# Attention of a two-layer decoder trunk: the transposes of both heads' probabilities moved beside those of the values, and a pair's outputs beside the scores of a later pair

## The chip, the cores and the metric

One core of one Trainium2 chip runs the whole program in one launch. The metric is the device time of one execution in microseconds (us). The kernel before has a median of 549.41 us over 3 runs (549.16 to 550.0).

## What is computed

The reference is a trunk of two layers over 256 tokens of width 1024, in float32: layer 0 mixes by causal pooling, layer 1 by attention, and each is followed by a squared-ReLU MLP. The change touches the attention of layer 1 alone. With 256 tokens there is one key block, so its sparse attention is plain causal attention over 16 heads of 64, with a bias by distance (cut):

```python
qkv = h @ w_qkv
logit = einsum('bhqd,bhkd->bhqk', q, k) * scale + bias_own      # causal: -inf above the diagonal
p = softmax(logit, axis=-1)
out = einsum('bhqk,bhkd->bhqd', p, v)
return out.reshape(B, S, D) @ w_o
```

## The kernel before, in words

All weights stream from memory and are split into a high and a low part (`w..._hi` by ACT on L247, `w..._lo` by DVE on L252), eight 128x128 tiles at a time and three such halves ahead of their use. A product with one weight tile is one **step**: three matmuls (L271 to L273). `next_tile()` counts the steps. `later(d, fn)` puts a function `d` steps on; what is due at a step is issued ahead of its three matmuls, in the order in which it was entered. Each engine runs its instructions in the order in which they were issued, so these numbers set the order of the work on PE, ACT and DVE, and nothing else does.

The products with `w_qkv` are 24 outputs of 8 steps. The heads go in eight pairs, and the outputs come in the order q, k of pair p, then v of pair p - 1, so that a pair takes 24 steps. The class `Pair` (from L898) hangs the attention of pair p between those steps:

- `done`: DVE takes an output out of its PSUM bank (L441, L443), and ACT turns it into q, k or the transposed v (L916: `qk`, `vT`).
- `scores` (10 steps after k): four matmuls in PE tiles of 64 rows and 128 columns into the banks `sc..._0` and `sc..._1` (L929). Then, spaced by steps, DVE adds the bias and takes the row maximum (`logits`, L944 and L949), ACT takes the exponentials with their sums (`exp`, L955), DVE the reciprocals (L960), and ACT multiplies by them (`normalize`, L966). The result stands in the tiles `L..._0` and `L..._1`.
- `transposes(e)` (25 and 26 steps after the scores): head e's probabilities are turned by three PE transposes into a bank `pt..._e` (L972). One step on, ACT copies them out to `PT..._e` (L974).
- `values` (9 steps after v is done): two PE transposes into the bank `pv` (L982), one step on ACT's copy to `v` (L984).
- `have`, called by both: when all is there, `outputs` follows 9 steps later, 5 for the last pair. It is four matmuls in PE tiles of 128 rows and 64 columns into the bank `po` (L996, L997), two steps on ACT's copy of the high part `ol` (L1001), one step on DVE's low part (L1004).

All banks come from one pool of eight. After the 192 steps of `w_qkv` the product with `w_o` begins. Its first five outputs `wo0` to `wo4` run side by side for 40 steps and hold five banks all that time, while the last two pairs are still being finished. Step counts below are from the scores of the pair, or of `w_o`.

Of the kernel before, what the change touches and what calls it, by code (L numbers as in the profile page):

```python
# [23 lines left out]
NP = H // 2  # L24
# [116 lines left out]
def tile_hybrid_pool_moba(  # L141
# [24 lines left out]
    def bank(name):  # L166
        return ps.tile([P, 512], F32, tag="ps", name=name)

    def al_tile(shape, name, dt=F32):
        return act.tile(shape, dt, tag="al", bufs=KF, name=name)  # L170
# [268 lines left out]
    def unnormed_out(b, R, name):  # L439
        u = tmp.tile([P, S], F32, tag="u", bufs=5, name=f"{name}_u")  # L440
        nc.vector.tensor_mul(u, b[:, :S], R)  # L441
        e = tmp.tile([P, 1], F32, tag="b", bufs=4, name=f"{name}_b")
        nc.vector.tensor_reduce(e, b[:, S:LO], axis=AX.X, op=ALU.add)  # L443
        return u, e
# [217 lines left out]
    def later(d, fn):  # L662
        due.setdefault(now[0] + d, []).append(fn)
# [22 lines left out]
    def up(layer, hl, R):  # L686
# [54 lines left out]
        for n, k in UP_ORDER[layer]:  # L741
            w = next_tile()
            paired = R is None and n < g and n % 2 == 1
            if k == 0:
                banks[n] = banks[n - 1] if paired else bank(f"{name}{n}")
            t = hl[k]
            if R is None:
                a = S if paired else 0

                last = n % 2 == 1 or n >= g  # L750
                args = (banks[n][:, a : a + S], w, t[:, :S], t[:, S : 2 * S], k == 0 and a == 0, k == KD - 1 and last)

                if k == 0 and n < HALF:
                    first_tiles.append(args)
                    if n == HALF - 1:
                        mm_sums(first_tiles)
                else:
                    mm_sum(*args)
            else:
                mm_sum(banks[n][:, :LO], w, t[:, :LO], t[:, LO : LO + S], k == 0, k == KD - 1)  # L760
            if k == KD - 1:
                done(n)
# [135 lines left out]
    class Pair:  # L898
# [15 lines left out]
        def done(self, j, b):  # L914
            u, e = unnormed_out(b, R[0], f"qkv{self.p}_{j}")
            later(1, lambda: nc.scalar.activation(self.dst(j), u, AF.Identity, bias=e))  # L916
            if j == 1:
                later(10, self.scores)
            if j == 2:
                later(9, self.values)  # L920

        def scores(self):
            p = self.p
            self.sc = [bank(f"sc{p}_{e}") for e in range(2)]
            for t in range(2):
                n = (t + 1) * P
                for e in range(2):
                    rows = slice(e * DH, (e + 1) * DH)
                    nc.tensor.matmul(  # L929
                        self.sc[e][:, t * P : t * P + n], self.qk[rows, 0, t * P : (t + 1) * P],  # L930
                        self.qk[rows, 1, S - n :], start=True, stop=True,
                    )
            self.prob = [al_tile([P, 2, (t + 1) * P], f"L{p}_{t}") for t in range(2)]
            for i, (t, e) in enumerate(((0, 0), (0, 1), (1, 0), (1, 1))):
                later(2 + i, lambda t=t, e=e: self.logits(t, e))
                later(10 + i, lambda t=t, e=e: self.exp(t, e))
                later(16 + i, lambda t=t, e=e: self.normalize(t, e))
            later(25, lambda: self.transposes(0))
            later(26, lambda: self.transposes(1))

        def logits(self, t, e):
            n = (t + 1) * P
# [43 lines left out]

        def have(self):
            if self.v is not None and len(self.PT) == 2:
                later(9 if self.p < NP - 1 else 5, self.outputs)

        def outputs(self):
            p = self.p
# [21 lines left out]
    for i, (n, k) in enumerate(QKV_ORDER):  # L1014
        w = next_tile()
        p, j = divmod(n, 3)
# [149 lines left out]
```

## Time and profile before

| what | us |
|---|---|
| median of 3 runs | 549.41 |
| the profiled execution, whole | 550.51 |
| its span (first to last instruction) | 548.7 |
| PE busy, share of the span | 537.5, 98% |
| DVE busy | 410.5, 75% |
| ACT busy | 323.6, 59% |
| the products with `w_qkv` on PE | 238.2 to 329.4 |
| the products with `w_o` begin | about 329.5 |

The profiled execution took 1.1 us longer than the median of the runs; 1.8 us of it lie around the span. Busy times of PE are of overlapping matmuls: a matmul is listed with some 0.28 us, and the next one starts 0.12 us after it. So what PE loses is read from start to start, not from its busy share.

### The profile page before, as it was taken

What the parts mean: (1) busy time and instruction counts of PE and PEld (TensorE: products, weight loads), DVE (VectorE), ACT (ScalarE), POOL (GpSimd) and SP (SyncE); (2) the same over time, 40 slices, a digit from 0 to 9 for tenths busy, and PEclk for the clock granted to TensorE, in tenths of its full rate; (3) what the DMA queues carried; (4) which work ended last, traced back from release to release, by engine and by line L of the source; (5) the groups of instructions that cost most, each with busy time, mean ns of one, the idle gap of its engine ahead of it and who ended that gap; (6) DMA issues with size and microseconds to landing.
All of it is one profiled execution on the core that took longest, in us unless ns stands there. A gap on an engine that the chain in (4) does not pass through costs nothing.

```text
span 548.7 us, 11124 instructions
## 1 busy us (share of the span) xinstructions
PE 537.5 (98%) x4492; PEld 499.5 (91%) x4492; DVE 410.5 (75%) x830; ACT 323.6 (59%) x605; POOL 2.5 (0%) x18
## 2 busy tenths in 40 slices
PE   8998999999999999999999999999999999999995
PEld 7777999999988888999999899999999998888895
DVE  2865598799889889966999994777887786665541
ACT  4224335789744445546988778566997774444531
POOL 1000000000000000000000000000000000000000
PEclk9997999999999999999999999999999999999998
DMA  8999989468999988974558774353565567676002
GB/s 335 416 420 406 360 321 380 177 231 300 318 383 392 382 334 324 351 254 153 189 213 297 289 288 163 121 206 141 177 226 173 212 230 260 221 263 254 1 1 76
DMA packets 22339, 140.43 MB, mean 256 GB/s; under 512 B 2416, under 2 KB 4608, under 8 KB 5904
## 3 DMA queue, kind: packets, MB, share of 16 engines
q1 hardware_dynamic: 22048, 138.61, 67.8%
q10 hardware_dynamic: 144, 1.05, 0.5%
q8 instruction: 35, 0.57, 0.4%
q14 instruction: 16, 0.13, 0.1%
q0 software_dynamic: 96, 0.06, 0.0%
HBM read 138.64 MB, written 1.07 MB: 255 GB/s over the span
## 4 chain that ended last, share of the span: by engine, by line
PE 92%; DMA 6%; DVE 0%; issue 0%; ACT 0%; DVEq 0%; ACTq 0%
PE m1d L264 9%; PE m0d L264 9%; PE m1u L271 6%; PE m1u L272 6%; PE m1u L273 6%; PE m0u L271 5%; PE m0u L273 5%; PE m0u L272 5%; PE m1d L265 5%; PE m0d L265 5%; PE qkv L271 5%; PE qkv L272 4%; PE qkv L273 4%; DMA raw_c_sh<-in_w_mod 3%; DMA raw_c_g<-in_w_mod 2%; PE wo L271 1%
## 5 line engine op out<-in xcount | busy, mean ns | idle before, releaser
L252 DVE TENSOR_TENSOR w_lo<-raw_w,w_hi 128x1024 fp32r<-128x1024 f32 x160 | 194.6, 1223 | 59.5 <-ACT w_hi L247 57.8
L247 ACT CAST w_hi<-raw_w 128x1024 fp32r<-128x1024 f32 x160 | 166.4, 1047 | 76.6 <-PE m1d L264 25.0
L264 PE MATMUL m1d<-m1u_al,w_hi 128*128 128x512 f32 x224 | 78.7, 394 | 0.0
L264 PE MATMUL m0d<-m0u_al,w_hi 128*128 128x512 f32 x224 | 78.1, 392 | 0.0
L295 DVE SCALAR_TENSOR_TENSOR raw_m<-raw_m,cact 128x1024 f32<-128x1024 f32 x62 | 75.3, 1218 | 0.0
L271 PE MATMUL m1u<-h_raw,w_hi 128*128 128x258 f32 x256 | 72.8, 284 | 0.0
L272 PE MATMUL m1u<-h_raw,w_hi 128*128 128x256 f32 x256 | 72.6, 284 | 0.0
L273 PE MATMUL m1u<-h_raw,w_lo 128*128 128x258 f32 x256 | 72.5, 283 | 0.0
L271 PE MATMUL m0u<-h,w_hi 128*128 128x256 f32 x248 | 69.8, 282 | 0.0
L273 PE MATMUL m0u<-h,w_lo 128*128 128x256 f32 x248 | 69.7, 281 | 0.0
L272 PE MATMUL m0u<-h,w_hi 128*128 128x256 f32 x248 | 69.4, 280 | 0.0
L265 PE MATMUL m1d<-m1u_al,w_lo 128*128 128x256 f32 x224 | 63.0, 281 | 0.0
L265 PE MATMUL m0d<-m0u_al,w_lo 128*128 128x256 f32 x224 | 62.8, 280 | 0.0
L271 PE MATMUL qkv<-h_raw,w_hi 128*128 128x258 f32 x192 | 57.4, 299 | 0.0
L272 PE MATMUL qkv<-h_raw,w_hi 128*128 128x256 f32 x192 | 54.6, 284 | 0.0
L273 PE MATMUL qkv<-h_raw,w_lo 128*128 128x258 f32 x192 | 54.4, 283 | 0.0
L264 PEld LDWEIGHTS m1d<-m1u_al,w_hi 128*128 128x128 f32 x224 | 42.1, 188 | 9.9
L264 PEld LDWEIGHTS m0d<-m0u_al,w_hi 128*128 128x128 f32 x224 | 42.1, 188 | 9.5
L273 PEld LDWEIGHTS m1u<-h_raw,w_lo 128*128 128x128 f32 x256 | 48.8, 191 | 0.0
L271 PEld LDWEIGHTS m1u<-h_raw,w_hi 128*128 128x128 f32 x256 | 48.7, 190 | 0.0
L272 PEld LDWEIGHTS m1u<-h_raw,w_hi 128*128 128x128 f32 x256 | 48.5, 190 | 0.0
L271 PEld LDWEIGHTS m0u<-h,w_hi 128*128 128x128 f32 x248 | 46.7, 188 | 0.9 <-issue 0.8
(179 smaller groups left out, 993.2 us busy)
## 6 DMA issues: line engine op xcount, KB each, us to landing
raw_w<-in_w_all SPq DMA_DIRECT2D x79, 1024.0 KB, 6.5
raw_m<-in_w_mod SPq DMA_DIRECT2D x31, 1024.0 KB, 6.8
raw_c_sh<-in_w_mod SPq DMA_DIRECT2D x8, 1024.0 KB, 13.6
raw_c_g<-in_w_mod SPq DMA_DIRECT2D x4, 1024.0 KB, 12.7
raw_c_mlp<-in_w_mod SPq DMA_DIRECT2D x4, 1024.0 KB, 10.7
T<-bd SPq DMA_DIRECT2D x8, 256.0 KB, 10.3
x<-in_xT ACTq DMA_DIRECT2D x1, 1024.0 KB, 5.9
wp<-in_w_pool SPq DMA_DIRECT2D x4, 256.0 KB, 14.1
```

Of the source, the lines that this page charges most:

```text
L247: nc.scalar.copy(hi, raw)
L252: nc.vector.tensor_sub(lo, raw, hi.bitcast(F32))
L264: nc.tensor.matmul(b, hi, hl[:, : 2 * S], start=start, stop=False)
L265: nc.tensor.matmul(b[:, S:], lo, hl[:, :S], start=False, stop=stop)
L271: nc.tensor.matmul(dst, hi, xh, start=start, stop=False)
L272: nc.tensor.matmul(dst[:, :S], hi, xl, start=False, stop=False)
L273: nc.tensor.matmul(dst, lo, xh, start=False, stop=stop)
L295: nc.vector.scalar_tensor_tensor(raw[:, a], raw[:, a], 1.0, cact, op0=ALU.mult, op1=ALU.mult, accum_out=dst[:, a : a + 1])
```

## The change

Four numbers that place work by steps are changed:

- The transposes of both heads' probabilities are due 31 steps after the pair's scores in place of 25 and 26. This is the step at which the values of the same pair are transposed (for the pairs 2 to 6; those of pairs 0 and 1, whose steps lie closer together, go next to nothing or by themselves). For the last pair they are due at 24.
- The values of the last pair are transposed 18 steps after v in place of 9, which is that same step.
- The outputs follow 17 steps after everything is there in place of 9, which is the step of the scores two pairs on. For the last pair it stays 5.

```diff
             if j == 2:
-                later(9, self.values)
+                later(9 if self.p < NP - 1 else 18, self.values)
...
-            later(25, lambda: self.transposes(0))
-            later(26, lambda: self.transposes(1))
+
+            for e in range(2):
+                later(31 if p < NP - 1 else 24, lambda e=e: self.transposes(e))
...
             if self.v is not None and len(self.PT) == 2:
-                later(9 if self.p < NP - 1 else 5, self.outputs)
+                later(5 if self.p == NP - 1 else 17, self.outputs)
```

The copies hang on the moved steps and move with them: `PT` one step after the transposes, `ol` two and three steps after the outputs. No instruction is added or taken away but for waits, and no transfer is moved. Lines from L938 on are one higher in the changed kernel.

PE around the scores of pair 5. A row is a matmul, output<-inputs with the pair's number in the name, and its size. Before, the outputs of pair 3 stand eight steps ahead of these scores (the steps between are left out):

```order
L273 MATMUL qkv4_2_3783<-h10_raw1_2275,w80_lo_3609 128x258
L996 MATMUL po3_3792<-PT3_0_3687,v3_3734 64x256
L997 MATMUL po3_3792<-PT3_0_3687,v3_3734 64x128
L996 MATMUL po3_3792<-PT3_1_3695,v3_3734 64x256
L997 MATMUL po3_3792<-PT3_1_3695,v3_3734 64x128
L271 MATMUL qkv4_2_3783<-h10_raw2_2377,w80_hi_3607 128x258
...
L273 MATMUL qkv6_0_3830<-h10_raw1_2275,w81_lo_3659 128x258
L929 MATMUL sc5_0_3839<-qk5_3735 128x128
L929 MATMUL sc5_1_3840<-qk5_3735 128x128
L929 MATMUL sc5_0_3839<-qk5_3735 128x256
L929 MATMUL sc5_1_3840<-qk5_3735 128x256
L271 MATMUL qkv6_0_3830<-h10_raw2_2377,w81_hi_3657 128x258
```

In the changed kernel:

```order
L273 MATMUL qkv6_0_3822<-h10_raw1_2275,w81_lo_3651 128x258
L997 MATMUL po3_3831<-PT3_0_3723,v3_3732 64x256
L998 MATMUL po3_3831<-PT3_0_3723,v3_3732 64x128
L997 MATMUL po3_3831<-PT3_1_3728,v3_3732 64x256
L998 MATMUL po3_3831<-PT3_1_3728,v3_3732 64x128
L929 MATMUL sc5_0_3836<-qk5_3733 128x128
L929 MATMUL sc5_1_3837<-qk5_3733 128x128
L929 MATMUL sc5_0_3836<-qk5_3733 128x256
L929 MATMUL sc5_1_3837<-qk5_3733 128x256
```

Outputs and scores touch, with no full-width matmul between them. This happens at four places: the outputs of pairs 2, 3, 4 and 5 ahead of the scores of pairs 4, 5, 6 and 7. The outputs of pairs 0 and 1 stand alone.

ACT between two casts of weights, where the exponentials of pair 5 lie. Before:

```order
L916 ACTIVATE vT4_3834<-qkv4_2_u_3821,qkv4_2_b_3823 128x256
L974 COPY PT4_0_3854<-pt4_0_3850 128x384
L974 COPY PT4_1_3862<-pt4_1_3858 128x384
L247 CAST w85_hi_3893<-raw_w_42_3655 128x1024
L916 ACTIVATE qk6_3907<-qkv6_0_u_3885,qkv6_0_b_3887 128x256
L984 COPY v4_3906<-pv4_3903 128x256
L955 ACTIVATE L5_0_3845,sm5_0_3919<-L5_0_3845,mx5_0_3869 128x128 x2
L955 ACTIVATE L5_1_3846,sm5_1_3930<-L5_1_3846,mx5_1_3880 128x256 x2
L247 CAST w86_hi_3946<-raw_w_43_3775 128x1024
L916 ACTIVATE qk6_3907<-qkv6_1_u_3941,qkv6_1_b_3943 128x256
```

In the changed kernel:

```order
L247 CAST w85_hi_3881<-raw_w_42_3647 128x1024
L916 ACTIVATE qk6_3905<-qkv6_0_u_3873,qkv6_0_b_3875 128x256
L975 COPY PT4_0_3895<-pt4_0_3891 128x384
L975 COPY PT4_1_3900<-pt4_1_3896 128x384
L985 COPY v4_3904<-pv4_3901 128x256
L956 ACTIVATE L5_0_3842,sm5_0_3919<-L5_0_3842,mx5_0_3857 128x128 x2
L956 ACTIVATE L5_1_3843,sm5_1_3930<-L5_1_3843,mx5_1_3868 128x256 x2
L247 CAST w86_hi_3946<-raw_w_43_3775 128x1024
L916 ACTIVATE qk6_3905<-qkv6_1_u_3941,qkv6_1_b_3943 128x256
```

The two copies of pair 4 have moved from ahead of a cast to between q of pair 6 and the exponentials of pair 5. It is so for the copies of pairs 2 to 5: each stands between q of the pair two on and the exponentials of the next pair. Those of pair 6 stand behind `vT7`, ahead of the exponentials of pair 7. On DVE the low part of the outputs (`ol`) now falls between the first and the second half of a pair's logits; before it stood behind a cast's low part.

PE at step 18 of `w_o`, where the last pair's probabilities are transposed. Before, `pv7` and `po6` had gone ahead of it, by ten and nine steps:

```order
L972 MATMUL pt7_0_4341<-vec_80,L7_0_4183 128x128
L972 MATMUL pt7_0_4341<-vec_80,L7_1_4184 128x128 x2
L271 MATMUL wo4_4259<-ol3_3805,w90_hi_4164 128x256
L272 MATMUL wo4_4259<-ol3_3805,w90_hi_4164 128x256
L273 MATMUL wo4_4259<-ol3_3805,w90_lo_4166 128x256
L972 MATMUL pt7_1_4349<-vec_80,L7_0_4183 128x128
L972 MATMUL pt7_1_4349<-vec_80,L7_1_4184 128x128 x2
```

In the changed kernel:

```order
L973 MATMUL pt7_0_4325<-vec_80,L7_0_4180 128x128
L973 MATMUL pt7_0_4325<-vec_80,L7_1_4181 128x128 x2
L973 MATMUL pt7_1_4330<-vec_80,L7_0_4180 128x128
L973 MATMUL pt7_1_4330<-vec_80,L7_1_4181 128x128 x2
L983 MATMUL pv7_4335<-vec_80,vT7_4240 128x128 x2
L997 MATMUL po6_4339<-PT6_0_4230,v6_4239 64x256
L998 MATMUL po6_4339<-PT6_0_4230,v6_4239 64x128
```

All the work of this place has moved into one step, one step ahead of where `pt7_0` was. Four tiles are opened at once while `wo0` to `wo4` hold five of the eight banks. In the built program `pt7_0` has bank 7, `pt7_1` bank 3, `pv7` bank 2, and `po6` bank 7 again, so its first matmul waits for ACT's copy `PT7_0`. That copy stands on ACT behind the last normalization of pair 7 and the cast `w93_hi`.

## Rows read from the trace of the kernel before

**Rows 1.** The page: the span, the busy times of the engines, and the chain that ended last by engine.
```profile
span 548.7 us, 11124 instructions
...
PE 537.5 (98%) x4492; PEld 499.5 (91%) x4492; DVE 410.5 (75%) x830; ACT 323.6 (59%) x605; POOL 2.5 (0%) x18
...
PE 92%; DMA 6%; DVE 0%; issue 0%; ACT 0%; DVEq 0%; ACTq 0%
```

**Rows 2.** Busy time by stretch, first and third of four stretches of one pair each, from the end of the scores of pair 3 to those of pair 4, and from pair 5 to pair 6: length of the stretch, then busy us (instructions) of PE, PEld, DVE, ACT and POOL, the granted clock, DMA share, GB/s.
```profile
279.99:291.64 11.65, 11.65 (x99) 10.72 (x97) 11.49 (x27) 9.84 (x25) 0.00 (x0) 1.00 0.77 283
...
303.29:314.93 11.64, 11.64 (x98) 10.71 (x96) 11.14 (x26) 9.01 (x22) 0.00 (x0) 1.00 0.78 288
```

**Rows 3.** PE in order of time: around the scores of pair 6, one head's transposes of pair 5, the transposes of the values of pair 5, and the outputs of pair 5. Columns: start us, duration us, engine, line, operation, output<-inputs, size; xN is N merged.
```profile
313.86 0.29 PE L273 MATMUL qkv<-h_raw,w_lo 128*128 128x258 f32 x1
314.08 0.93 PE L929 MATMUL sc<-qk 64*128 64x128 f32 x8
314.93 0.39 PE L271 MATMUL qkv<-h_raw,w_hi 128*128 128x258 f32 x1
315.16 0.28 PE L272 MATMUL qkv<-h_raw,w_hi 128*128 128x256 f32 x1
315.28 0.29 PE L273 MATMUL qkv<-h_raw,w_lo 128*128 128x258 f32 x1
315.40 0.49 PE L972 MATMUL pt<-vec,L 128*128 128x128 f32 x3
...
315.85 0.28 PE L272 MATMUL qkv<-h_raw,w_hi 128*128 128x256 f32 x1
...
318.11 0.29 PE L273 MATMUL qkv<-h_raw,w_lo 128*128 128x258 f32 x1
...
318.58 0.28 PE L272 MATMUL qkv<-h_raw,w_hi 128*128 128x256 f32 x1
...
321.60 0.29 PE L273 MATMUL qkv<-h_raw,w_lo 128*128 128x258 f32 x1
321.82 0.66 PE L996 MATMUL po<-PT,v 128*64 128x256 f32 x4
...
322.85 0.28 PE L272 MATMUL qkv<-h_raw,w_hi 128*128 128x256 f32 x1
```

**Rows 4.** DVE in order of time, from the logits of pair 5 to those of pair 6; in brackets the idle time before an instruction and what ended it.
```profile
304.63 0.48 DVE L944 SCALAR_TENSOR_TENSOR L<-sc,T 128x128 f32<-128x128 f32 x2
...
306.86 0.41 DVE L441 TENSOR_TENSOR qkv_u<-qkv,n_R 128x256 f32<-128x256 f32 x1
...
309.73 0.38 DVE L960 RECIPROCAL rs<-sm 128x2 f32<-128x2 f32 x2
310.03 0.40 DVE L441 TENSOR_TENSOR qkv_u<-qkv,n_R 128x256 f32<-128x256 f32 x1
...
312.69 0.42 DVE L1004 TENSOR_TENSOR ol<-po,ol 128x256 fp32r<-128x256 f32 x1
313.46 0.42 DVE L441 TENSOR_TENSOR qkv_u<-qkv,n_R 128x256 f32<-128x256 f32 x1 [0.34 <-PE qkv L273]
...
316.33 0.48 DVE L944 SCALAR_TENSOR_TENSOR L<-sc,T 128x128 f32<-128x128 f32 x2
```

**Rows 5.** ACT in order of time in the same stretch: q of pair 6, the copy of v of pair 4, the first exponential of pair 5, the last read-out of its sums, k of pair 6, the two copies of pair 5's transposed probabilities.
```profile
307.38 0.51 ACT L916 ACTIVATE qk<-qkv_u,qkv_b 128x256 f32<-128x256 f32 x1
307.80 0.36 ACT L984 COPY v<-pv 128x256 f32<-128x256 f32 x1
308.05 0.40 ACT L955 ACTIVATE L<-L,mx 128x128 f32<-128x128 f32 x1
...
309.73 0.19 ACT L955 ACTIVATION_READ_ACCUMULATOR L<-L,mx 128x1 f32 x1
...
310.75 0.51 ACT L916 ACTIVATE qk<-qkv_u,qkv_b 128x256 f32<-128x256 f32 x1
...
315.93 0.48 ACT L974 COPY PT<-pt 128x384 f32<-128x384 f32 x1 [1.14 <-PE pt L972]
316.62 0.48 ACT L974 COPY PT<-pt 128x384 f32<-128x384 f32 x1 [0.21 <-PE pt L972]
```

**Rows 6.** ACT in order of time at the end: the transposed v of pair 7, the copy of its v, `ol` of pair 6, the last normalization of pair 7, the cast `w93_hi`, and the two copies of its transposed probabilities.
```profile
330.55 0.50 ACT L916 ACTIVATE vT<-qkv_u,qkv_b 128x256 f32<-128x256 f32 x1
...
335.73 0.35 ACT L984 COPY v<-pv 128x256 f32<-128x256 f32 x1
...
336.69 0.35 ACT L1001 CAST ol<-po 128x256 fp32r<-128x256 f32 x1
336.94 0.51 ACT L966 ACTIVATE L<-L,rs 128x256 f32<-128x256 f32 x1
337.35 1.04 ACT L247 CAST w_hi<-raw_w 128x1024 fp32r<-128x1024 f32 x1
338.29 1.07 ACT L974 COPY PT<-pt 128x384 f32<-128x384 f32 x2
```

**Rows 7.** DVE in the same stretch: the sum that v of pair 7 waits for.
```profile
330.05 0.15 DVE L443 TENSOR_REDUCE qkv_b<-qkv 128x1 f32<-128x2 f32 x1
```

**Rows 8.** PE in the same stretch: the transposes of pair 7's probabilities, head 0 and head 1.
```profile
337.68 0.49 PE L972 MATMUL pt<-vec,L 128*128 128x128 f32 x3
...
338.36 0.49 PE L972 MATMUL pt<-vec,L 128*128 128x128 f32 x3
```

## The prediction

> **What bounds the kernel now.** I read the page first. PE is busy for 537.5 of 548.7 us and holds 92% of the chain that ended last, with 6% for transfers at the start [rows 1]. So a change in the attention counts by what it does to the time from one PE start to the next, and work of ACT or DVE counts where PE comes to wait for it.
>
> Then the stretches of one pair each. A pair takes 11.64 to 11.65 us, and PE has no gap in it. But DVE is busy for 11.14 to 11.49 us of it, and ACT for 9.01 to 9.84 [rows 2]. DVE has almost no room; ACT has two microseconds.
>
> The order of time on PE shows what the small matmuls cost. Ordinary matmuls start 0.12 us apart (315.16 to 315.28). I measure from the L273 ahead of a group to the L272 behind it and take off 0.24 for two ordinary distances [rows 3]. The scores cost 315.16 - 313.86 - 0.24 = 1.06, the outputs 322.85 - 321.60 - 0.24 = 1.01, three transposes 315.85 - 315.28 - 0.24 = 0.33, and two 0.23. A transpose costs 0.11, and a group of them nothing on top. Scores and outputs do have something on top: the first starts 0.22 behind the L273 (314.08, 321.82), 0.10 more than ordinary, and behind them L272 starts 0.23 after L271 (314.93 to 315.16), 0.11 more. These seams go with the change of PE's tile, 64x128 and 128x64 beside 128x128.
>
> The orders of time on DVE and ACT show a loop between them. From the logits of pair 5 to those of pair 6 DVE takes 316.33 - 304.63 = 11.70, and in it waits 0.34 for PE [rows 4]. Near its middle the reciprocals need ACT's exponentials. The last sums are read out by 309.73 + 0.19 = 309.92 [rows 5]; the two reciprocals take 0.38 from 309.73, one alone 0.17 (310.11 less 0.17 is 309.94) [rows 4]. So the second one waits for ACT already, and whatever comes ahead of the exponentials on ACT delays DVE at once. Before, the copies of the transposed probabilities stood where ACT was idle for 1.14 and 0.21 [rows 5].
>
> **The change, part by part.**
>
> *Outputs against scores.* At four places two groups touch, and the inner seams go: 0.11 behind the outputs and 0.10 ahead of the scores. The direct change from 128x64 to 64x128 is not in the trace. It saves nothing if it costs both seams and 0.21 if it costs none; I take 0.15, between those and a change that costs like one seam. That is 4 x 0.15 = 0.6 us less PE time (bounds 0 and 0.84).
>
> The Trainium skill, "TensorEngine Tiling (Array Packing)", Key Properties, says that a change of the tiling mode drains the engine. By it the step from outputs to scores is still such a change, one drain goes in place of two, and the gain would be nearer 0.4. No row here shows the direct change.
>
> *Transposes together.* Eight in a row in place of 3, 3 and 2: 0.33 + 0.33 + 0.23 against 8 x 0.11. Nothing.
>
> *Copies ahead of the exponentials.* The two copies of a pair are listed with 0.48 each [rows 5]. Back to back an ACT instruction starts about 0.09 before the listed end of the one ahead (307.80 against 307.38 + 0.51), so two take 0.77. They now stand between q and the copy of v, ahead of five sets of exponentials (pairs 3 to 7). The DVE loop becomes longer by 0.77 and can give back only its 0.34 of waiting for PE: 11.70 - 0.34 + 0.77 = 12.13, against 11.64 - 0.15 = 11.49 that PE would now need. DVE's low part of the outputs stays in the loop, at another place. The loop bounds the stretch, and DVE falls back by 0.43 per pair against the trace before. From the logits of pair 3 to those of pair 7 these are four loops, 1.7 us. k of a pair was ready at 310.75 + 0.51 [rows 5] and its scores began at 314.08 [rows 3], 2.8 us of slack; that covers most of it, so I expect only short waits at the last scores.
>
> *The end of the attention.* Here it reaches PE. The transposed v of pair 7 needs a sum that DVE had by 330.20 [rows 7], while ACT came to it at 330.55 [rows 6]: 0.35 of slack. So it starts 1.7 - 0.35 late. Between it and the last normalization of pair 7 the copies of pair 6 come in (0.77), and the copy of v of pair 7 and `ol` of pair 6 go out (0.25 each, as 336.69 to 336.94). The last normalization starts 1.7 - 0.35 + 0.77 - 0.50 = 1.6 later than 336.94. Then come the cast and the copy `PT7_0`, which began 338.29 - 336.94 = 1.35 behind it [rows 6] and takes 0.48. It ends at 336.94 + 1.6 + 1.35 + 0.48 = 340.4.
>
> Now `po6`, in step 18, may start only then, since it has the bank of `pt7_0`. Where was PE before when it had the same work behind it? At 337.68 it began `pt7_0` [rows 8] with `pv7` and `po6` done. Take off a step (3 x 0.12 = 0.36) and `po6` (1.01), and add the six transposes (0.66): 336.97. PE is late by 340.4 - 336.97 = 3.4 us.
>
> The Trainium skill, "PSUM — Partial Sum Buffer", Engine vs sequencer instructions, says that the queues of ScalarE and VectorE are strictly first in, first out. By it the copy cannot pass the cast ahead of it. If it could, the wait would end some 0.9 earlier and the sum would be 2.5. In the trace ACT runs in the order of its program, which agrees.
>
> *Sum.* What PE gains before this place only lengthens its wait there, so neither the 0.6 nor short waits at scores or at the banks of `wo1` and `wo4` are added. Behind it nothing is late: `po7` comes a `po` and five steps later, 2.8 us, and its copies need under one. The split weights are made three halves of eight steps ahead (24 x 0.36 = 8.6 us), so DVE's lag of 2 does not reach them; no transfer moves. The change costs **3.4 us**. The profiled execution took 550.5 and should become 553.9; it lay 1.1 above the median, and from that 549.4 + 3.4 = **552.8**.
>
> **The rivals.**
>
> *A, the loop costs more.* If DVE's wait for PE isn't given back (it comes behind the place where DVE is held), each loop loses 0.77: 3.1 in place of 1.7, and PE is 4.8 late: 554.2. For it speaks that DVE had only 11.65 - 11.49 = 0.16 to give at pair 3 [rows 2]; against it the 0.34 at pair 5. It decides if PE waits for k at the scores of pairs 5 to 7.
>
> *B, only the end counts.* If DVE catches up between the pairs, ACT's chain moves with PE: 0.6 earlier, 0.77 and -0.50 as above. `PT7_0` ends at 338.77 - 0.33 = 338.4, and PE is 1.5 late: 550.9. ACT's two free microseconds per pair speak for it, the second reciprocal against it.
>
> *C, not slower.* ACT has `PT7_0` copied when PE arrives, and only the seams are left: 549.4 - 0.6 = 548.8. For this the copy must end by 336.97 - 0.6 = 336.4, that is 2.4 us earlier than the 338.77 of before. From the transposed v on, ACT shows no idle time in its rows, and the change adds 0.27 to them. PE's lead alone does not give 2.4.
>
> **Numbers.** A measurement of this kernel can tell 0.2%, 1.1 us, from no change. Forecast 0.60, A 0.16, B 0.17, C 0.07. The forecast, A and most of B lie above 550.5: slower 0.88. C and the rest of B are the same, 0.09; faster, 0.03, needs the upper bound of the seams and C together. The range leaves out C and the lower end of B, and above it a lag beyond A: 550.5 to 555.0.
>
> **What would show it.** In the profile after, PE should stand still in the first steps of `w_o` for about 3 to 4 us in all, most of it at the last transposes and at `po6`, with ACT named as the releaser. DVE's waits for L956 should rise by several tenths per pair, and its wait for PE in front of L441 should vanish. ACT's idle time ahead of the copies (1.14 and 0.21) should be gone. From outputs to scores PE should go in less than the 1.06 + 1.01 of both. I am wrong if PE shows no gap around `po6`, if DVE's distance from logits to logits stays at 11.7 or below, or if PE waits most at scores.

## The result, and the profile after

The changed kernel takes 552.8 us (median of 6 runs) beside 549.7 for the kernel before in the same runs: a ratio of 1.0056, with a 95% interval of 1.0042 to 1.007, or 3.1 us slower (2.3 to 3.8). The forecast was 552.8, with a range of 550.5 to 555.0. That the forecast and the median agree to the digit is partly luck: the median of before was 549.4 over the first three runs and 549.7 over six, and the trace shows a loss larger than 3.4.

To compare two traces I count from the first matmul with `w_qkv` to the first matmul of the MLP behind `w_o`; the same work lies between in every kernel here. The two ends before:

```profile
238.15 0.29 PE L271 MATMUL qkv<-h_raw,w_hi 128*128 128x258 f32 x1
...
355.27 0.28 PE L271 MATMUL m1u<-h_raw,w_hi 128*128 128x258 f32 x1
```

and after:

```profile
236.50 0.29 PE L271 MATMUL qkv<-h_raw,w_hi 128*128 128x258 f32 x1
...
357.43 0.28 PE L271 MATMUL m1u<-h_raw,w_hi 128*128 128x258 f32 x1
```

This is 117.12 us before and 120.93 after, 3.81 more. The whole spans differ by less (550.6 and 548.7), since the first `w_qkv` matmul came 1.65 us earlier in the profiled run of after. That lead is there already when the first MLP begins (51.9 against 53.6 us), ahead of all that the change touches. To set a time of after beside one of before, 1.65 is added to it.

The page of the changed kernel, beside [rows 1]:

```profile
span 550.6 us, 11133 instructions
...
PE 537.1 (98%) x4492; PEld 499.0 (91%) x4492; DVE 410.1 (74%) x830; ACT 322.4 (59%) x605; POOL 2.5 (0%) x18
...
PE 78%; DVE 9%; DMA 6%; ACT 5%; issue 1%; DVEq 0%; ACTq 0%
```

PE does the same work (537.1 us), but holds 78% of the chain where it held 92%; DVE has 9% and ACT 5%. For a while PE is no longer what everything waits for.

PE in order of time at the end of the attention. In brackets: the idle time before, and what ended it.

```profile
324.23 0.93 PE L929 MATMUL sc<-qk 64*128 64x128 f32 x8 [0.51 <-ACT qk L916]
...
329.09 0.36 PE L271 MATMUL wo<-ol,w_hi 128*128 128x256 f32 x1 [0.35 <-DVE ol L1005]
...
330.87 0.36 PE L271 MATMUL wo<-ol,w_hi 128*128 128x256 f32 x1 [0.48 <-DVE qkv_b L443]
...
336.85 0.33 PE L973 MATMUL pt<-vec,L 128*128 128x128 f32 x1 [0.80 <-ACT L L967]
337.54 0.84 PE L973 MATMUL pt<-vec,L 128*128 128x128 f32 x5 [0.36 <-ACT L L967]
338.21 0.38 PE L983 MATMUL pv<-vec,vT 128*128 128x128 f32 x2
339.25 0.66 PE L997 MATMUL po<-PT,v 128*64 128x256 f32 x4 [0.65 <-ACT PT L975]
```

Here are PE's waits of the last two pairs, one after another: the scores of pair 7 (0.51), `wo1` (0.35), `wo4` (0.48), the last transposes (0.80 and 0.36), `po6` (0.65). Before, not one of these was listed. From start to start, less what is ordinary, they cost 0.56, 0.59, 0.64, 0.95, 0.58 and 0.71. (Ordinary for `wo1` is 0.13: in the kernel before, a `w_o` step starts that much behind the first of two transposes of values, 329.99 against 329.86.) A seventh, 0.44, is at the scores of pair 3 (below). That is 4.5 us of standing still; 0.8 comes back at the places where outputs and scores touch, which leaves 3.7 of the 3.81.

The stretches of one pair in the same kernel, from the end of the scores of pair 4 to those of pair 5 and from 5 to 6, columns as in [rows 2]:

```profile
290.17:301.61 11.44, 11.44 (x99) 10.66 (x97) 10.39 (x24) 8.04 (x23) 0.00 (x0) 1.00 0.66 233
301.61:313.08 11.47, 11.47 (x98) 10.66 (x97) 10.56 (x26) 8.13 (x22) 0.00 (x0) 1.00 0.78 279
```

PE takes 11.44 and 11.47 where it took 11.65: for these pairs the change gives what it promises. DVE is less busy than before (10.39 and 10.56), so it waits more. DVE in order of time from the logits of pair 5 to those of pair 6, beside [rows 4]:

```profile
304.47 0.48 DVE L945 SCALAR_TENSOR_TENSOR L<-sc,T 128x128 f32<-128x128 f32 x2
...
305.31 0.41 DVE L1005 TENSOR_TENSOR ol<-po,ol 128x256 fp32r<-128x256 f32 x1
...
309.90 0.15 DVE L961 RECIPROCAL rs<-sm 128x2 f32<-128x2 f32 x1
310.86 0.17 DVE L961 RECIPROCAL rs<-sm 128x2 f32<-128x2 f32 x1 [0.80 <-ACT L L956]
...
313.61 0.41 DVE L441 TENSOR_TENSOR qkv_u<-qkv,n_R 128x256 f32<-128x256 f32 x1
...
316.48 0.48 DVE L945 SCALAR_TENSOR_TENSOR L<-sc,T 128x128 f32<-128x128 f32 x2
```

The distance is 316.48 - 304.47 = 12.01 us where it was 11.70. The second reciprocal waits 0.80 for ACT's exponentials; the wait of 0.34 for PE is gone. PE needs 11.47 for the pair and DVE 12.01, so DVE falls back. ACT in the same stretch, beside [rows 5], shows why:

```profile
307.54 0.51 ACT L916 ACTIVATE qk<-qkv_u,qkv_b 128x256 f32<-128x256 f32 x1 [2.52 <-DVE qkv_b L443]
307.96 0.84 ACT L975 COPY PT<-pt 128x384 f32<-128x384 f32 x2
308.69 0.38 ACT L985 COPY v<-pv 128x256 f32<-128x256 f32 x1
308.95 0.42 ACT L956 ACTIVATE L<-L,mx 128x128 f32<-128x128 f32 x1
```

The two copies take 308.69 - 307.96 = 0.73 between q of pair 6 and the copy of v, and the exponentials wait behind them, while ACT had been idle for 2.52 ahead of that q. It is ACT's order that costs here, not its load.

ACT at the end, beside [rows 6]:

```profile
330.76 0.51 ACT L916 ACTIVATE vT<-qkv_u,qkv_b 128x256 f32<-128x256 f32 x1 [2.26 <-DVE qkv_b L443]
331.17 0.84 ACT L975 COPY PT<-pt 128x384 f32<-128x384 f32 x2
...
336.40 1.49 ACT L967 ACTIVATE L<-L,rs 128x128 f32<-128x128 f32 x4
337.79 1.04 ACT L247 CAST w_hi<-raw_w 128x1024 fp32r<-128x1024 f32 x1
338.73 0.84 ACT L975 COPY PT<-pt 128x384 f32<-128x384 f32 x2
```

The transposed v of pair 7 starts at 330.76, with 1.65 at 332.41 instead of 330.55: 1.86 late. The copies of pair 6 lie behind it, and the last normalization (the fourth of the merged row, 0.51 ahead of its end) starts at 337.38, or 339.03, 2.1 late. Then come the cast and `PT7_0`, which ends at 338.73 + 0.48 = 339.21; `po6` starts at 339.25.

The waits of DVE for the exponentials, summed up from `w_qkv` to the attention's end (us in all, times, the longest), before:

```profile
DVE rs L960 <- ACT L L955: 2.8, 6, 0.8
```

and after:

```profile
DVE rs L961 <- ACT L L956: 6.7, 8, 1.2
```

### The profile page after: what moved, and what is told of

Its sections match the earlier page's. It is cut to its first block, busy times and chain, and to the rows that moved or that the text cites. A ratio compares the mean times of both kernels' runs of the same rounds, so it can differ in the third digit from the quotient of the medians.

```text
span 550.6 us, 11133 instructions
## 1 busy us (share of the span) xinstructions
PE 537.1 (98%) x4492; PEld 499.0 (91%) x4492; DVE 410.1 (74%) x830; ACT 322.4 (59%) x605; POOL 2.5 (0%) x18
## 3 DMA queue, kind: packets, MB, share of 16 engines
q10 hardware_dynamic: 144, 1.05, 0.5%
## 4 chain that ended last, share of the span: by engine, by line
PE 78%; DVE 9%; DMA 6%; ACT 5%; issue 1%; DVEq 0%; ACTq 0%
PE m1d L264 9%; PE m0d L264 9%; PE m1u L271 6%; PE m1u L272 6%; PE m1u L273 6%; PE m0u L271 5%; PE m0u L273 5%; PE m0u L272 5%; PE m1d L265 5%; PE m0d L265 5%; DMA raw_c_sh<-in_w_mod 3%; DVE w_lo L252 2%; DMA raw_c_g<-in_w_mod 2%; DVE raw_m L295 2%; ACT L L956 2%; DVE L L945 1%
## 5 line engine op out<-in xcount | busy, mean ns | idle before, releaser
L272 PE MATMUL m1u<-h_raw,w_hi 128*128 128x256 f32 x256 | 72.6, 284 | 0.0
L273 PE MATMUL m1u<-h_raw,w_lo 128*128 128x258 f32 x256 | 72.5, 283 | 0.0
L273 PE MATMUL m0u<-h,w_lo 128*128 128x256 f32 x248 | 69.7, 281 | 0.0
L272 PE MATMUL m0u<-h,w_hi 128*128 128x256 f32 x248 | 69.4, 280 | 0.0
L271 PE MATMUL qkv<-h_raw,w_hi 128*128 128x258 f32 x192 | 56.1, 292 | 0.0
L272 PE MATMUL qkv<-h_raw,w_hi 128*128 128x256 f32 x192 | 54.6, 284 | 0.0
L273 PE MATMUL qkv<-h_raw,w_lo 128*128 128x258 f32 x192 | 54.4, 283 | 0.0
L273 PEld LDWEIGHTS m1u<-h_raw,w_lo 128*128 128x128 f32 x256 | 48.8, 191 | 0.0
L272 PEld LDWEIGHTS m1u<-h_raw,w_hi 128*128 128x128 f32 x256 | 48.5, 190 | 0.0
```

The source lines that it names most:

```text
L271: nc.tensor.matmul(dst, hi, xh, start=start, stop=False)
L272: nc.tensor.matmul(dst[:, :S], hi, xl, start=False, stop=False)
L273: nc.tensor.matmul(dst, lo, xh, start=False, stop=stop)
```

## The experiments

The theory: (1) ACT's copies ahead of the exponentials lengthen the loop between DVE and ACT; (2) at the end, PE meets ACT late, and `po6` in the bank of `pt7_0` waits for the last link of the chain. The rivals were R1, that only the end counts and the pairs do no harm; R2, that the moved outputs are to blame, through DVE's low part of them between the halves of the logits; and R3, that the shared bank is of no account. Every kernel computes the whole of the reference. The table has all runs: the ratio to the kernel before and its interval; the stretch from `w_qkv` to the MLP as above; and DVE's distances from the logits of pair 4 to 5 and from 5 to 6.

| kernel | ratio, 95% interval | stretch, us | against before | logits 4 to 5, 5 to 6 |
|---|---|---|---|---|
| before | 1 | 117.12 | | 11.27, 11.70 |
| changed | 1.0056 (1.0042 to 1.007) | 120.93 | +3.81 | 12.01, 12.01 |
| e1, outputs only | 0.9992 (0.9979 to 1.0004) | 116.40 | -0.72 | 11.27, 11.27 |
| e2, transposes only | 1.0029 (1.0017 to 1.004) | 119.13 | +2.01 | 12.02, 12.01 |
| e3, last pair as before | 1.0019 (1.0007 to 1.0031) | 118.88 | +1.76 | 12.02, 12.02 |
| e4, copies behind the exponentials | 1.0045 (1.0027 to 1.0063) | 119.21 | +2.09 | 11.27, 11.35 |
| e5, outputs of pair 6 early | 1.0029 (1.0017 to 1.0041) | 119.47 | +2.35 | 12.01, 12.01 |
| e6, copies alone | 1.0011 (1.0001 to 1.0021) | 118.39 | +1.27 | 12.01, 12.01 |
| e7, all outputs | 0.9972 (0.9962 to 0.9981) | 116.07 | -1.05 | 11.27, 11.26 |
| e8, e3 and e4 together | 0.9981 (0.9967 to 0.9994) | 117.04 | -0.08 | 11.26, 11.35 |

An interval of the ratio is 0.5 to 1.0 us to either side, so for sizes I read the stretch. It comes from one profiled execution of each kernel. How well it repeats shows in the five kernels that are alike up to the 98th step of `w_qkv` (changed, e3, e4, e5, e8): they take 44.95 to 44.99 us to there. Behind the attention the stretch's difference stays as it is, within 0.1, through the MLP's first product; in the last product every profile gains 0.1 to 0.6 us on that of before. From the end of the stretch to the end of the span it is 193.43 us before, 193.17 after, 193.45 in e1 and 192.8 to 193.1 in the other experiments. The cause of this is open. By the stretch alone e3, e5, e6 and e8 lie outside the intervals of their ratios, all four on the slower side; with the part behind it added, every kernel lies inside (3.55 for the change, 1.20, 1.76, 0.88 and -0.62 for these four).

**e1, the outputs alone** (against before):

```diff
-                later(9 if self.p < NP - 1 else 5, self.outputs)
+                later(5 if self.p == NP - 1 else 17, self.outputs)
```

> Only the outputs move (17 steps after everything is there, so beside the scores two pairs on); the probabilities' transposes stay at 25 and 26 and the values of the last pair at 9, as before. Theory (the copies of the transposed probabilities, placed ahead of the exponentials, lengthen the loop of DVE and ACT, and the lag reaches PE at the end): the copies stay where ACT had room, so the DVE distance from logits to logits stays at 11.3 to 11.7 us, PE waits nowhere, and four contacts at about 0.19 each come off: 0.5 to 0.9 us faster than before, some 549.0. Rival R2 (the moved outputs are to blame, because DVE's low part of them now falls between the two halves of a pair's logits): 1 us or more slower than before, with PE waiting for k at the scores.

By the stretch 0.72 us faster; the ratio alone would also allow no change. No wait of PE is listed (a hidden one of 0.34, shown under e7, is here too), and the loop stays at 11.27. R2 falls: DVE's low part between the halves of the logits costs nothing that shows.

**e2, the transposes alone** (against the change):

```diff
-                later(5 if self.p == NP - 1 else 17, self.outputs)
+                later(9 if self.p < NP - 1 else 5, self.outputs)
```

> Only the transposes move (31, for the last pair 24, its values 18); the outputs stay 9 steps behind, so the outputs of pair 6 go eight steps ahead of the last transposes and want no bank then. Theory: the copies stand ahead of the exponentials, the loop is 0.3 to 0.8 us per pair longer, and PE waits at the first outputs of w_o and at the last transposes, but not at the outputs of pair 6: 1.2 to 2.2 us slower than before, 550.9 to 551.9. Rival R1 (the pairs do no harm, only four groups in one step with three free banks cost): within 0.5 us of before. Rival R2 (the outputs are to blame): within 0.5 us of before.

1.6 us slower by the ratio, 2.01 by the stretch, with DVE's loop at 12.01. So the transposes carry a loss without any outputs moved, and R1 in its plain form falls, since `po6` has a bank of its own here. Not all of the 2.01 is the theory's: from step to step PE loses 0.55 at the outputs of pair 0 (1.56 where 1.01 is ordinary), which here come before ACT has copied that pair's transposed probabilities, 0.3 at the outputs of pair 5, which wait for the copy of v, 0.4 at `wo4` and 0.9 at the last transposes. The changed kernel, with its outputs later, has neither of the first two, and e1 and e2 do not add up to it.

**e3, the last pair as before, and e4, the copies behind the exponentials** (each against the change):

```diff
-                later(9 if self.p < NP - 1 else 18, self.values)
+                later(9, self.values)
...
-                later(31 if p < NP - 1 else 24, lambda e=e: self.transposes(e))
+                later(31 if p < NP - 1 else 25 + e, lambda e=e: self.transposes(e))
```

```diff
-            later(1, lambda: nc.scalar.copy(PT, pt[:, : 3 * P]))
+            later(6 if 1 < p < NP - 1 else 1, lambda: nc.scalar.copy(PT, pt[:, : 3 * P]))
```

> The change, but for the last pair the transposes at 25 and 26 and the values at 9, as before: the outputs of pair 6 then find a bank, and nothing of the last pair is gathered in one step. Theory: the lag of DVE and ACT stays, with the waits at the scores (0.9 us in all) and at wo1 and wo4 (1.1), less the contacts (0.75), and a short wait for the last normalization: 1.0 to 1.9 us slower than before, some 551.2. Rival R1 (only the end counts): 0.5 to 0.9 us faster than before, 549.0.

> The change, with one thing put elsewhere: for pairs 2 to 6 ACT's two copies of the transposed probabilities come 6 steps after the transposes in place of 1, so that they stand behind the exponentials of the next pair. Theory: DVE's wait for the sums (0.80 us a pair in the changed kernel) falls to below 0.4, the distance from logits to logits to about 11.5, the waits at the scores of pair 7, at wo1 and at wo4 go, and what is left is the step with the last transposes and the outputs of pair 6: 1.0 to 1.8 us slower than before, 550.7 to 551.5. Rival R1 (only the end counts): no better than the changed kernel, 3 us slower than before, 552.8.

With e8, which has both edits, these make a table of two by two. With the copies ahead of the exponentials: 3.81 with the new last pair, 1.76 with the old one. With the copies behind: 2.09 and -0.08. The place of the copies costs 1.7 or 1.8 us, whichever the end; the last pair's step costs 2.1 or 2.2, whichever the copies. Both parts of the theory are there, and in these four traces they add (with the part behind the stretch it is 1.8 and 1.8, 2.3 and 2.4). The ratios (3.1, 1.0, 2.5 and -1.0 us) agree in direction, but are too coarse for it: by them the copies' place costs about 2 beside the old last pair and 0.6, with 1.2 to either side, beside the new one.

PE's waits in e3 (us in all, times, the longest) are those of the loop alone:

```profile
PE sc L929 <- ACT qk L916: 0.9, 2, 0.5
PE wo L271 <- DVE qkv_b L443: 0.5, 1, 0.5
PE wo L271 <- DVE ol L1005: 0.3, 1, 0.3
```

In e4 these are gone but for one wait at the scores of pair 3 (0.38), and DVE's waits for the exponentials fall back:

```profile
DVE rs L961 <- ACT L L956: 3.3, 6, 0.8
```

What e4 keeps is the step with the last transposes. PE in order of time in e4:

```profile
335.57 0.33 PE L973 MATMUL pt<-vec,L 128*128 128x128 f32 x1 [0.79 <-ACT L L967]
336.26 0.83 PE L973 MATMUL pt<-vec,L 128*128 128x128 f32 x5 [0.36 <-ACT L L967]
...
337.97 0.66 PE L997 MATMUL po<-PT,v 128*64 128x256 f32 x4 [0.66 <-ACT PT L975]
```

and ACT:

```profile
329.48 0.51 ACT L916 ACTIVATE vT<-qkv_u,qkv_b 128x256 f32<-128x256 f32 x1 [1.10 <-DVE qkv_b L443]
...
335.11 1.49 ACT L967 ACTIVATE L<-L,rs 128x128 f32<-128x128 f32 x4
336.51 1.03 ACT L247 CAST w_hi<-raw_w 128x1024 fp32r<-128x1024 f32 x1
337.44 0.86 ACT L975 COPY PT<-pt 128x384 f32<-128x384 f32 x2
```

PE waits there as long as in the changed kernel (0.79, 0.36 and 0.66 against 0.80, 0.36 and 0.65). Without the lag both PE and ACT come 1.8 earlier, and the distance between them stays. That is why e4 cost more than I expected (1.0 to 1.8 us; 2.09 by the stretch, 2.5 by the ratio): I had let ACT's chain at the end start 0.6 earlier than in the kernel before, along with PE. The transposed v started at 329.48, which is 330.65 on the clock of before, against 330.55. DVE, not PE, sets it.

**e5, the outputs of pair 6 early** (against the change):

```diff
-                later(5 if self.p == NP - 1 else 17, self.outputs)
+                later({NP - 1: 5, NP - 2: 9}.get(self.p, 17), self.outputs)
```

> The change, but for pair 6 the outputs come 9 steps behind in place of 17: eight steps ahead of the last transposes, with a bank of their own. Theory: the wait for ACT's copy out of the shared bank (0.65 us listed) goes, and the 1.01 us of these outputs fill what was waiting for the last normalization; the waits of the pairs stay: 1.3 to 1.8 us less than the changed kernel, that is 1.3 to 2.1 us slower than before, some 551.4. Rival R3 (the bank is of no account, because PE would wait for ACT's last normalization as long): within 0.5 us of the changed kernel.

2.35 by the stretch, just above my range, and 1.46 less than the change; 1.6 by the ratio. Of the three waits in the step one is still listed, and part of another shows in the length of the row (1.10 for five transposes that took 0.84):

```profile
337.61 1.10 PE L973 MATMUL pt<-vec,L 128*128 128x128 f32 x5 [0.35 <-ACT L L967]
```

So the shared bank did count, and R3 falls: 0.71 of the 1.46 is the wait at `po6`. For the rest, PE now does the four matmuls ahead of the step, in time that it would have spent waiting for the normalization.

**e6, the copies alone** (against before):

```diff
-            later(1, lambda: nc.scalar.copy(PT, pt[:, : 3 * P]))
+            later((7 if e == 0 else 6) if 1 < p < NP - 1 else 1, lambda: nc.scalar.copy(PT, pt[:, : 3 * P]))
```

> The kernel before, and nothing moves on PE: only ACT's two copies of the transposed probabilities of pairs 2 to 6 come 6 and 7 steps later, which puts them between q of the pair two on and the exponentials of the next pair, as in the change. Theory: the loop alone gets longer, DVE waits about 0.8 us per pair for the sums, and PE is late at the last transposes: 0.7 to 1.6 us slower than before, 550.4 to 551.3. Rivals R1 and R2 (the end, or the outputs, are to blame): within 0.4 us of before.

The order on PE stays, and DVE's loop goes from 11.27 and 11.70 to 12.01 and 12.01, with these waits for the exponentials in all:

```profile
DVE rs L960 <- ACT L L955: 6.6, 8, 1.2
```

1.27 us slower by the stretch. By the ratio it is 0.6, with an interval from 0.1 to 1.2: below my range by the value, but slower. That the copies' place alone makes the loop longer is shown; in time it is near what these runs can tell. PE loses only part of it where the changed kernel did: 0.42 at `wo4` and 0.27 at the last transposes. The other 0.25 and 0.38 are at the outputs of pairs 4 and 5, which wait for ACT's copy of v, and that copy now stands behind the two moved ones. At pair 5:

```profile
321.43 0.66 PE L996 MATMUL po<-PT,v 128*64 128x256 f32 x4 [0.30 <-ACT v L984]
```

**e7, the outputs where the theory would have them** (against before; those of pairs 0 and 1 go together beside the scores of pair 3):

```diff
-                later(9 if self.p < NP - 1 else 5, self.outputs)
+                later({0: 20, 1: 10, NP - 2: 9, NP - 1: 5}.get(self.p, 17), self.outputs)
```

> The outputs alone, as the theory would place them: those of pairs 2 to 5 beside the scores of 4 to 7, those of pairs 0 and 1 together beside the scores of 3, those of pair 6 at 9 as before, all transposes and copies as before. Theory: six contacts between groups in place of none, about 0.19 us each, with no wait for ACT or DVE: 0.9 to 1.3 us faster than before, some 548.6. If three groups in one step hold up banks or DVE: no faster than 549.2.

548.56 us beside 550.1: 1.5 us faster by the ratio (1.0 to 2.1), 1.05 by the stretch. This version beats both kernels. PE in order of time where two outputs and scores touch:

```profile
276.44 0.66 PE L997 MATMUL po<-PT,v 128*64 128x256 f32 x4
...
277.14 0.65 PE L997 MATMUL po<-PT,v 128*64 128x256 f32 x4
...
277.94 0.93 PE L929 MATMUL sc<-qk 64*128 64x128 f32 x8
```

The two groups of outputs start 0.70 apart, the scores 0.80 behind the second. Not all of it is kept: without `po0` ahead of them, the second transposes of pair 1 come too early for ACT, which costs 0.34 (listed with 0.83 where 0.49 is usual):

```profile
272.06 0.83 PE L973 MATMUL pt<-vec,L 128*128 128x128 f32 x3
```

**e8, the copies and the last pair** (against the change, the edits of e3 and e4 together):

> The change with both suspected places mended: the copies of pairs 2 to 6 behind the exponentials and the last pair's numbers as before; the transposes stay beside those of the values, the outputs beside the scores. Theory: loop and end explain all of the loss, so what is left is the four contacts less a wait of 0.4 at the scores of pair 3: 0.1 to 0.7 us faster than before, some 549.3. If the transposes beside the values cost something by themselves: slower than before.

Faster than before by the ratio, by 0.3 to 1.8 us, its value of 1.0 beyond my range; by the stretch no more than even, 0.08, just short of it. Of the 0.8 of the contacts, 0.44 go at the scores of pair 3, and 0.36 at the last transposes of head 0 (0.85 where 0.49 is usual):

```profile
335.86 0.85 PE L973 MATMUL pt<-vec,L 128*128 128x128 f32 x3
```

So nothing large is left to explain, and the transposes beside those of the values do no harm once the copies have their place; but nothing shows that they bring anything. e1, which leaves them where they were, is the faster of the two by the stretch, e8 by the ratio; it isn't settled.

## Why the prediction was right, step by step

**Outputs against scores.** Forecast 0.15 at each of four places, measured 0.20. PE around the outputs of pair 2 and the scores of pair 4 in the changed kernel:

```profile
288.29 0.29 PE L273 MATMUL qkv<-h_raw,w_lo 128*128 128x258 f32 x1
288.51 0.66 PE L997 MATMUL po<-PT,v 128*64 128x256 f32 x4
288.99 0.39 PE L998 MATMUL po<-PT,v 128*64 128x128 f32 x4
289.32 0.93 PE L929 MATMUL sc<-qk 64*128 64x128 f32 x8
290.17 0.39 PE L271 MATMUL qkv<-h_raw,w_hi 128*128 128x258 f32 x1
290.40 0.28 PE L272 MATMUL qkv<-h_raw,w_hi 128*128 128x256 f32 x1
```

From L273 ahead to L272 behind, less 0.24, the two groups cost 290.40 - 288.29 - 0.24 = 1.87, and apart they cost 1.06 + 1.01 = 2.07 [rows 3]. That is the upper value that I allowed for the seams I had counted. The change between the modes is not free, though: outputs followed by scores take 289.32 - 288.51 = 0.81, and in e7 outputs followed by outputs 277.14 - 276.44 = 0.70. A third seam of 0.11, behind the last matmul of a group, had been hidden in the group's price. So the rule of the Trainium skill ("TensorEngine Tiling (Array Packing)", Key Properties), that a change of the tiling mode drains the engine, agrees with the trace, 0.11 for this change; but a contact saved 0.20, and the gain was 0.8, not 0.4.

**The loop.** Right in its mechanism; the term was too small. I put the loop at 12.13 and the lag at 0.43 per pair, 1.7 for four. The four loops measured 12.34, 12.01, 12.01 and 11.20, against 11.60, 11.27, 11.70 and 10.86 before: 0.74, 0.74, 0.31 and 0.34 more, 2.1 in all. I had read both the loop of 11.70 and the room that DVE could give back (0.34) at pair 5 and used them for every pair. Room of that size was there in the last two loops only, and in the last one not at a wait for PE (0.23 of it is a wait for ACT's cast `w_hi`, 0.47 before and 0.24 after); the first two lost the full 0.74 of the copies, as rival A had it. That rival would have needed it at all four.

**The scores.** I expected short waits at the last ones. That of pair 7 was 0.51. The one of 0.44 at pair 3 I had not seen: PE has the outputs of pairs 0 and 1 still ahead of it and comes to these scores 2.1 us earlier than before, while ACT begins k only 0.7 earlier (275.30 with 1.65, against 277.61). e8 has that wait too, without the lag.

**The end.** The last normalization was to start 1.6 late and was 2.1 late; the extra 0.5 is the lag's (1.86 at the transposed v, where I had 1.35). `PT7_0` was to end at 340.4 and ended at 339.21 + 1.65 = 340.86; PE was to be 3.4 late and was 3.8. The waits at `wo1` and `wo4` that I left out of the sum came, 1.2 us. They were rightly left out: where the end waits for ACT, they only take the place of more waiting there, and what the copies' place costs is the same with either end (1.7 and 1.8). By the Trainium skill ("PSUM — Partial Sum Buffer", Engine vs sequencer instructions) the queue of ScalarE is first in, first out; ACT in e4 agrees: the copy at 337.44 comes directly behind the cast of 336.51.

**The rivals.** B, with no lag, is what e4 does. It came to 2.1 late, not 1.5, for the reason given there. C needed ACT's copy 2.4 us earlier, and it came 2.1 later. "Slower" was safe: each of the two parts alone made the kernel slower (e3, e4).

**The signs I named.** In the first steps of `w_o` PE stood still for 3.5 us, 2.2 of it at the last transposes and at `po6` with ACT as the releaser; DVE's waits for the exponentials rose from 2.8 to 6.7 in all; its wait for PE went, and so did ACT's idle time ahead of the copies.

## What to carry to other kernels

Before moving work on the engine that bounds the kernel, look where the helpers' instructions that hang on it will stand in their own queues: here a copy of 0.4 us cost nothing where its engine was idle, and up to its whole length inside a loop that another engine waits for. Gathering PE's small groups paid only at seams, here where the tile mode changes; the full-width transposes have none (0.11 each), so nothing was to be won by putting them together. And a bank that was opened and used again within one step turned a copy that was off the path into one that the bounding engine waits for.

## What the runs showed of the hardware

The outputs, four matmuls in tiles of 64 columns, cost PE about 0.1 us three times beside their own 0.70: ahead of the first (0.22 from start to start where 0.12 is ordinary), behind the last (0.81 instead of 0.70), and behind the first full-width matmul after them (0.23 instead of 0.12). The scores, in tiles of 64 rows, show the first and the third of these; the second has no row to compare with. Where outputs and scores touch, one of the three is left between them; where outputs touch outputs (e7), none.
